# Low score product of a two-part attention kernel: full-height zero-padded matmuls replaced by half-height row tiles of TensorE

## Chip, cores, metric

The kernel runs on one core of one Trainium2 chip. The metric is the device time of one execution in microseconds; the runs before the change gave a median of 685.42 us (three runs, 685.2 to 685.59). The profile is one further execution, taken by the hardware profiler.

## What is computed

One layer of a streaming encoder: layer norm with a modulation, one input projection, two attention branches of 8 heads each, a gate, one output projection, a residual and a second layer norm. Sequence length and width are 1024, the head dimension 64, the query block 128, all in float32. Cut to the two branches around the change (`ke` is the number of keys that query block `i` sees):

```python
for i in range(8):
    qs, ke = i * 128, (i + 1) * 128
    # stick-breaking branch
    z = einsum('bhqd,bhkd->bhqk', q[:, :, qs:ke], k[:, :, :ke]) * 64 ** -0.5
    log_keep = where(strict, log_sigmoid(-z), 0)
    later = cumsum(log_keep, reverse=True) - log_keep
    w = where(strict, exp(log_sigmoid(z) + later), 0);  out = w @ v
    # forgetting branch
    s = einsum(...) * 64 ** -0.5 + (f_q[:, None] - f_k[None, :])
    out = softmax(where(causal, s, -inf)) @ v
```

## The kernel before

**Two-part numbers.** Most matmuls here take their operands in a rounded float32 type (`fp32r`). To keep the accuracy, the kernel splits each operand in a rounded high part and the rest, the low part, and adds up products of the parts: high times high, low times high, high times low.

**Pairs and units.** The 16 heads are treated as 8 pairs `p` of two heads `h`; pairs 0 to 3 are the stick-breaking heads, 4 to 7 the forgetting ones. A *unit* is `(p, h, i)`: one head and one block of 128 queries, with `ke = 128 * (i + 1)` keys, 128 units in all. Half of them (`i` of 0 to 3) have at most 512 keys, half have 640, 768, 896 or 1024.

**Where q and k stand.** For each head, `qst[p][h]` and `kst[p][h]` are tiles of 128 partitions by 1024 columns. `evac_q` (L265) puts the high part of q on the partition half of its own head, `r`, and the low part on the other half, `o`. `evac_k` (L274) puts the high part of k on half `r`, copies it by a DMA to half `o`, and writes the low part to `klo[p]`, one tile for both heads, each on its own half and at its own key columns (L284). One product of 128 rows, `qst` by `kst`, then gives high q by high k plus low q by high k at once (L459).

**The low product before.** What is left is high q by low k. `klo[p]` holds both heads, one on each half, so the stationary operand is a padded tile: `qz[h][b]` (two buffers per head) is cleared at the start (L104), and `att_query` (L428) copies the high q of the unit, 64 partitions by 128 columns, to the half of its head (L433, on ScalarE, 128 times). The other half stays zero, and a 128-row product (L460) with `klo[p]` gives the head's share alone.

**How a unit goes.** `att_scores` (L447) writes the scores of a unit to `S`, a PSUM tile of two banks of 512 columns, of which there is one. Up to 512 keys take one bank. More keys are cut into two equal halves, one per bank: width 320, 384, 448 or 512 each, in the order high, low, high, low. Then ScalarE takes the sigmoids `kp` and `be` from S (L481, L483; pairs 0 to 3), or VectorE takes the masked sum and maximum (L467; pairs 4 to 7). VectorE scans `kp` (L488), or ScalarE takes the exponential (L472); POOL multiplies (L494, L475). Two units later, PE transposes the weights in blocks of 128 (L511), ScalarE and VectorE split them in two parts (L513, L514), and PE multiplies them by v (L528).

**What sets the order.** On PE the order is the written one: after each unit's scores come projection matmuls of later pairs as fillers (L296 to L298, L354 to L356; a table `FILL` says how many steps per pair), transposes and products with v. Near the end the fillers are the output projection (L913 to L915). On SP the order is written by hand for the start. On ScalarE, VectorE and POOL a scheduler of the framework sets it from its own model of time. In pair 4 and later, the forget gates' row sums are transposed once by a matmul that uses 64 columns of the array (L411, tile `frow`).

Of the kernel before, what the change touches and what calls it, by code (L numbers as in the profile page):

```python
# [8 lines left out]
F32 = mybir.dt.float32  # L9
F32R = mybir.dt.float32r  # L10
AF = mybir.ActivationFunctionType
ALU = mybir.AluOpType

P = 128
# [4 lines left out]
HD = 64  # L19
# [8 lines left out]
def tile_hybrid_layer(  # L28
# [17 lines left out]
    nc = tc.nc  # L46
# [9 lines left out]
    def att_tile(name, dt=F32):  # L56
        return big("att", 6, name, dt)
# [13 lines left out]
    def s_tile(name):  # L71
        return ps.tile([P, 2, 512], F32, tag="S", bufs=1, name=name)
# [10 lines left out]
    def after(*instructions):  # L83
        stack = ExitStack()
        for i in instructions:
            stack.enter_context(tc.issue_after(i.ins))
        return stack
# [11 lines left out]
    nc.gpsimd.memset(half.bitcast(F32), 0.5)  # L99

    qz = [[cp.tile([P, P], F32R, tag=f"qz{h}{b}", name=f"qz{h}{b}") for b in range(2)] for h in range(2)]
    for h in range(2):
        for t in qz[h]:
            nc.gpsimd.memset(t.bitcast(F32), 0.0)  # L104
    gate = cp.tile([P, D], F32, tag="gate", name="gate")
    mhalf = cp.tile([P, 1], F32, tag="mhalf", name="mhalf")
    nc.gpsimd.memset(mhalf, -0.5)
# [73 lines left out]
    for kt in range(NB):  # L181
        nc.tensor.matmul(sc_all[:, kt // 4, kt % 4 * P:][:, :P], sc[:, kt:kt + 1].to_broadcast([P, P]), ident,
                         start=True, stop=True)
# [90 lines left out]
    def evac_k(p, ch, acc, kst, klo, heads):  # L274
        s = slice(ch * 512, ch * 512 + 512)
        for h in heads:
            r = slice(h * HD, h * HD + HD)
            o = slice((1 - h) * HD, (1 - h) * HD + HD)
            first = nc.scalar.copy(kst[h][r, s], acc[r, :])
            if ch == 1 and p in (2, 4, 6):  # L280
                key_casts[:] = [first]
            kf = kst[h].bitcast(F32)
            nc.sync.dma_start(kf[o, s], kf[r, s])
            last = nc.vector.tensor_tensor(klo[r, s], acc[r, :], kf[r, s], op=ALU.subtract)  # L284
        return first, last

    def evac_g(p, ch, acc, sg):
# [12 lines left out]
    qst, kst, klo, sgt, vt = {}, {}, {}, {}, {}  # L300
# [12 lines left out]
    def evac_m(p, m, ch, acc, heads=(0, 1)):  # L313
        if m == 0:
            evac_q(p, ch, acc, qst[p], heads)
        elif m == 1:
            return evac_k(p, ch, acc, kst[p], klo[p], heads)
        else:
            evac_g(p, ch, acc, sgt[p])
# [108 lines left out]
    def att_query(u):  # L428
        p, h, i = u
        zq[u] = z = qz[h][turn[h] % 2]  # L430
        turn[h] += 1
        r = slice(h * HD, h * HD + HD)
        nc.scalar.copy(z[r, :], qst[p][h].bitcast(F32)[r, i * P:i * P + P])  # L433

    masks, scaled, lows = [], [], []

    def att_causal(u):
        p, h, i = u
        if p >= 4:
            if not masks:  # L440
                masks.append(pv_tile("causal_ps", 1)[:, :P])
                nc.vector.tensor_copy(masks[0], causal)
            f = fb[2 * (p - 4) + h]
            dg = slice(i * P, i * P + P)
            nc.vector.tensor_tensor(f[:, dg], f[:, dg], masks[0], op=ALU.add)

    def att_scores(u, following):  # L447
        p, h, i = u
        z = zq.pop(u)
        ke = (i + 1) * P  # L450
        ns = 1 if ke <= 512 else 2
        w = ke // ns
        qs = slice(i * P, i * P + P)
        if p >= 4:
            f = fb[2 * (p - 4) + h]
        S = s_tile(f"S_{p}_{h}_{i}")
        for s in range(ns):
            ks = slice(s * w, s * w + w)
            nc.tensor.matmul(S[:, s, :w], qst[p][h][:, qs], kst[p][h][:, ks], start=True, stop=False)  # L459
            nc.tensor.matmul(S[:, s, :w], z, klo[p][:, ks], start=False, stop=True)  # L460
        v3 = lambda a: a[:, :ke].rearrange("p (a b) -> p a b", a=ns)
        if p >= 4:
            a = att_tile(f"a_{p}_{h}_{i}")
            nm = sb.tile([P, 1], F32, tag="nm", bufs=4, name=f"nm_{p}_{h}_{i}")
            l = sb.tile([P, 1], F32, tag="l", bufs=4, name=f"l_{p}_{h}_{i}")
            with after(*lows):
                nc.vector.tensor_tensor_reduce(out=v3(a), in0=S[:, :ns, :w], in1=v3(f),  # L467
                                               op0=ALU.add, op1=ALU.min, scale=-1.0, scalar=BIG,
                                               accum_out=nm)
            if following:  # L470
                att_causal(following)
            nc.scalar.activation(a[:, :ke], a[:, :ke], AF.Exp, scale=-1.0, bias=nm, accum_out=l)  # L472
            nc.vector.reciprocal(l, l)  # L473
            scaled[:] = [*scaled[-3:],
                         nc.gpsimd.tensor_scalar(a[:, :ke], a[:, :ke], l, 1.0, op0=ALU.mult, op1=ALU.mult)]  # L475
            st_w[u] = a
        else:
            kp = att_tile(f"kp_{p}_{h}_{i}")
            be = att_tile(f"be_{p}_{h}_{i}")
            with after(*key_casts):  # L480
                nc.scalar.activation(v3(kp), S[:, :ns, :w], AF.Sigmoid, scale=-1.0)  # L481
            key_casts.clear()
            last_act = nc.scalar.activation(v3(be), S[:, :ns, :w], AF.Sigmoid)  # L483


            lo = max(ke - 512, 0)
            rv = kp[:, lo:ke][:, ::-1]
            last_dve = nc.vector.tensor_tensor_scan(rv, rv, floor[:, :ke - lo], initial=0.0,  # L488
                                                    op0=ALU.mult, op1=ALU.max)
            if lo:  # L490
                rv = kp[:, :lo][:, ::-1]
                last_dve = nc.vector.tensor_tensor_scan(rv, rv, floor[:, P:P + 1].to_broadcast([P, lo]),  # L492
                                                        initial=kp[:, lo:lo + 1], op0=ALU.mult, op1=ALU.max)
            nc.gpsimd.tensor_tensor(be[:, :ke - 1], be[:, :ke - 1], kp[:, 1:ke], op=ALU.mult)  # L494
            nc.gpsimd.memset(be[:, ke - 1:ke], 0.0)
            st_w[u] = be
            return last_act, last_dve
# [182 lines left out]
    for kb in range(NB):  # L680
        last = kb == NB - 1
# [17 lines left out]
        else:  # L699
            parts = range(2 if kb + 2 < NB else 0)  # L700
# [110 lines left out]
    for kb in range(NB):  # L811
# [9 lines left out]
        if kb < len(evacs):  # L821
            n, h = evacs[kb]
# [6 lines left out]
    last = nc.vector.tensor_copy(held[:, 512:], acc1[1])  # L829
# [230 lines left out]
    def scores_turn(k):  # L1060
        if k < len(units):
            if k == 16 * 4 - 1:
                load_fb(0)
                load_fb(1)
            if k == 0:
                att_query(units[0])
            issued = att_scores(units[k], units[k + 1] if k + 1 < len(units) else None)
            if k == 16 * 4 - 1:
                att_causal(units[k + 1])
            if k in HELD:  # L1070
                m, h = HELD[k]
                with after(*issued):
                    evac_m(0, m, 1, held[:, m * 512:(m + 1) * 512], (h,))
            with after(*(issued or ())):
                while summed:
                    att_sum(*summed.pop(0))
            if k + 1 < len(units):
                att_query(units[k + 1])
            p, h, i = units[k]
            if 4 <= p < NPAIR - 1 and i == 0:  # L1080
                load_fb(2 * (p - 4) + h + 2)
# [83 lines left out]
```

## Time and profile before

| what | value |
|---|---|
| median of 3 runs | 685.42 us (685.2 to 685.59) |
| the profiled execution's own time | 685.27 us |
| its span, first to last instruction | 683.2 us |
| mean granted TensorE clock | 0.998 |
| instructions | 11185 |
| matmuls and weight loads | 3713 each |
| HBM | 60.34 MB read, 16.29 MB written |

PE is the row of matmuls, PEld that of the loads of stationary operands, which run beside PE. DVE is VectorE, ACT ScalarE, POOL GpSimd. In a timeline row stand start and length in us, engine, line, operation, the tile written and the tiles read, then `rows*columns` of the array and the moving operand, whose second number is the width. Matmuls are pipelined: the next one can start before the record of the last one ends. The chain that ended last follows the work back from the last instruction, at each step to what released it.

### The profile page before, as it was taken

How to read it: one execution, taken by the hardware profiler on the slowest of the kernel's cores; microseconds unless marked ns; L12 is line 12 of the kernel's file. 1: busy time of each engine (PE TensorE's matmuls, PEld its weight loads, DVE VectorE, ACT ScalarE, POOL GpSimd, SP SyncE). 2: the span in 40 equal slices, each digit the busy share in tenths (PEclk: the TensorE clock that was granted, in tenths of full speed). 3: DMA queues.
4: the chain of work that ended last, by engine and by line, in shares of the span. 5: the costliest groups of instructions: out<-in, count | busy, mean ns of one | idle time of the engine just before them, and what ended most of it. 6: DMA issues, size and time to landing. Idle time of an engine off the chain costs nothing.

```text
span 683.2 us, 11185 instructions
## 1 busy us (share of the span) xinstructions
PE 670.8 (98%) x3713; PEld 571.9 (84%) x3713; DVE 485.1 (71%) x996; ACT 379.1 (55%) x857; POOL 404.6 (59%) x529
## 2 busy tenths in 40 slices
PE   8999999999999999999999999999999999999995
PEld 4788898888998888889988888889988888888885
DVE  6697779878666777786776675766676777875645
ACT  5567377756567666575665565655565666521000
POOL 5560179756357656566378878777785365655411
PEclk9999999999999999999999999999999999999999
DMA  9973422112102121122123455254352297143301
GB/s 330 410 274 141 140 74 79 29 39 59 32 15 65 45 64 42 40 54 55 49 92 129 166 161 169 79 173 147 117 163 73 61 356 300 59 178 104 119 32 61
DMA packets 45272, 81.54 MB, mean 119 GB/s; under 512 B 5216, under 2 KB 19360, under 8 KB 44960
## 3 DMA queue, kind: packets, MB, share of 16 engines
q1 hardware_dynamic: 43632, 76.54, 34.3%
q10 hardware_dynamic: 1584, 4.31, 1.9%
q8 instruction: 29, 0.48, 0.3%
q14 instruction: 27, 0.22, 0.1%
HBM read 60.34 MB, written 16.29 MB: 112 GB/s over the span
## 4 chain that ended last, share of the span: by engine, by line
PE 91%; DVE 2%; POOL 2%; ACT 2%; issue 1%; DMA 1%; SPq 0%; DVEq 0%; POOLq 0%; ACTq 0%
PE m L296 10%; PE m L298 10%; PE m L297 9%; PE pv L528 9%; PE T L511 9%; PE S L459 5%; PE S L460 5%; PE o L915 4%; PE o L913 4%; PE o L914 4%; PE v L356 4%; PE v L354 4%; PE v L355 4%; PE st_q L620 1%; PE st_late L620 1%
## 5 line engine op out<-in xcount | busy, mean ns | idle before, releaser
L514 DVE TENSOR_TENSOR pt<-T,pt 128x512 fp32r<-128x512 f32 (+2 forms) x192 | 102.8, 552 | 31.6 <-ACT pt L513 30.0
L296 PE MATMUL m<-uh,whi 128*128 128x512 f32 x304 | 122.8, 404 | 0.0
L513 ACT CAST pt<-T 128x512 fp32r<-128x512 f32 (+2 forms) x192 | 88.7, 478 | 58.9 <-PE T L511 54.9
L298 PE MATMUL m<-uh,wlo 128*128 128x512 f32 x304 | 119.7, 394 | 0.0
L297 PE MATMUL m<-ul,whi 128*128 128x512 f32 x304 | 119.6, 393 | 0.0
L494 POOL TENSOR_TENSOR be<-be,kp 128x127 f32<-128x127 f32 (+3 forms) x64 | 78.4, 1226 | 37.0 <-DVE kp L492 23.9
L488 DVE TENSOR_TENSOR_SCAN kp<-kp,floor 128x512 f32<-128x512 f32 (+2 forms) x64 | 65.0, 1015 | 26.3 <-ACT kp L481 25.1
L528 PE MATMUL pv<-pt,v 128*128 128x512 f32 x320 | 82.8, 389 | 0.0
L459 PE MATMUL S<-k,q 128*128 128x512 f32 (+5 forms) x192 | 69.4, 363 | 0.3 <-DVE nm L467 0.2
L475 POOL TENSOR_SCALAR a<-a,l 128x1024 f32<-128x1024 f32 (+3 forms) x64 | 48.1, 752 | 36.4 <-DVE l L473 26.8
L298 PEld LDWEIGHTS m<-uh,wlo 128*128 128x128 f32 x304 | 57.1, 188 | 13.7
L296 PEld LDWEIGHTS m<-uh,whi 128*128 128x128 f32 x304 | 57.1, 188 | 10.2
L460 PE MATMUL S<-kl,qz 128*128 128x512 f32 (+5 forms) x192 | 65.3, 341 | 0.0
L297 PEld LDWEIGHTS m<-ul,whi 128*128 128x128 f32 x304 | 57.2, 188 | 9.4
L472 ACT ACTIVATE a<-a,nm 128x1024 f32<-128x1024 f32 (+3 forms) x64 | 49.8, 778 | 26.7 <-DVE nm L467 26.1
L528 PEld LDWEIGHTS pv<-pt,v 128*128 128x128 f32 x320 | 55.5, 189 | 9.0
L544 POOL TENSOR_TENSOR ty<-ty,sg 64x256 f32<-64x256 f32 x64 | 47.0, 734 | 23.3 <-DVE ty L543 10.0
L467 DVE CUSTOM_DVE_ANT_0 a<-S,fb 128x1024 f32<-128x1024 f32 (+3 forms) x64 | 48.2, 753 | 16.2 <-PE S L460 12.0
L433 ACT CAST qz<-q 64x128 fp32r<-64x128 f32 x128 | 37.3, 296 | 34.1 <-PE S L460 32.8
L356 PE MATMUL v<-wlo_v,uh 128*128 128x256 f32 (+1 forms) x192 | 54.4, 283 | 0.8 <-POOL wlo_v L127 0.8
L354 PE MATMUL v<-whi_v,uh 128*128 128x256 f32 (+1 forms) x192 | 54.7, 285 | 0.0
L355 PE MATMUL v<-whi_v,ul 128*128 128x256 f32 (+1 forms) x192 | 54.1, 282 | 0.0
(290 smaller groups left out, 1609.8 us busy)
## 6 DMA issues: line engine op xcount, KB each, us to landing
raw<-in_w_qkg_dram SPq DMA_DIRECT2D x38, 256.0 KB, 2.7
wss<-in_w_ss_dram SPq DMA_DIRECT2D x12, 512.0 KB, 8.5
x<-in_x_dram SPq DMA_DIRECT2D x8, 512.0 KB, 7.3
k<-k SPq DMA_DIRECT2D x32, 128.0 KB, 2.3
wg<-in_w_gate_dram SPq DMA_DIRECT2D x8, 512.0 KB, 5.0
raw_o<-in_w_out_dram SPq DMA_DIRECT2D x16, 256.0 KB, 3.0
fb<-f_dr ACTq DMA_DIRECT2D x8, 512.0 KB, 4.3
wo_dr<-whi_o SPq DMA_DIRECT2D x16, 256.0 KB, 2.2
```

Of the source, the lines that this page charges most:

```text
L296: nc.tensor.matmul(acc, hi[:, c], u_hi[kt][:, s], start=(kt == 0), stop=False)
L297: nc.tensor.matmul(acc, hi[:, c], u_lo[kt][:, s], start=False, stop=False)
L298: nc.tensor.matmul(acc, lo[:, c], u_hi[kt][:, s], start=False, stop=(kt == NB - 1))
L354: nc.tensor.matmul(acc[:, :n], u_hi[kt][:, ts_], hi[:, s], start=(kt == 0), stop=False)
L355: nc.tensor.matmul(acc[:, :n], u_lo[kt][:, ts_], hi[:, s], start=False, stop=False)
L356: nc.tensor.matmul(acc[:, :n], u_hi[kt][:, ts_], lo[:, s], start=False, stop=(kt == NB - 1))
L459: nc.tensor.matmul(S[:, s, :w], qst[p][h][:, qs], kst[p][h][:, ks], start=True, stop=False)
L460: nc.tensor.matmul(S[:, s, :w], z, klo[p][:, ks], start=False, stop=True)
L494: nc.gpsimd.tensor_tensor(be[:, :ke - 1], be[:, :ke - 1], kp[:, 1:ke], op=ALU.mult)
L513: nc.scalar.copy(hi[:, :n, qo:qo + P], t3)
L514: lows[:] = [nc.vector.tensor_tensor(lo[:, :n, qo:qo + P], t3, hi.bitcast(F32)[:, :n, qo:qo + P], op=ALU.subtract)]
L528: nc.tensor.matmul(acc2[:, :, q0:], vt[p][:, kb, h * P:(h + 1) * P], pt[:, :, q0:], start=(kb == 0), stop=(kb == last))
```

## The change

1. `klo[p]` is laid out by key half: head `h` takes columns `512 h` to `512 h + 511`, with its first 512 keys on partitions 0 to 63 and the other 512 on partitions 64 to 127.
2. More than 512 keys are cut into 512 and the rest (128, 256, 384 or 512), no longer into equal halves; the columns of S are now contiguous.
3. All high products of a unit come first, then the low ones. A low product has 64 rows: for key part `s` those of partition half `s`. On the head's own half (`s == h`) the stationary operand is `qst` itself; on the other it is a copy of the high q, moved to that half.
4. `att_query` makes that copy only where it is needed: not for head 0 with `i` below 4, whose keys all lie in part 0. So 96 of the 128 copies stay. The padding is gone, and with it the four memsets.

```diff
-    for h in range(2):
-        for t in qz[h]:
-            nc.gpsimd.memset(t.bitcast(F32), 0.0)
...
-            last = nc.vector.tensor_tensor(klo[r, s], acc[r, :], kf[r, s], op=ALU.subtract)
+            last = nc.vector.tensor_tensor(klo[ch * HD:ch * HD + HD, h * 512:h * 512 + 512], acc[r, :], kf[r, s],
+                                           op=ALU.subtract)
...
+        if h == 0 and i < 4:
+            return
         r = slice(h * HD, h * HD + HD)
-        nc.scalar.copy(z[r, :], qst[p][h].bitcast(F32)[r, i * P:i * P + P])
+        o = slice((1 - h) * HD, (1 - h) * HD + HD)
+        nc.scalar.copy(z[o, :], qst[p][h].bitcast(F32)[r, i * P:i * P + P])
...
-        for s in range(ns):
-            ks = slice(s * w, s * w + w)
-            nc.tensor.matmul(S[:, s, :w], qst[p][h][:, qs], kst[p][h][:, ks], start=True, stop=False)
-            nc.tensor.matmul(S[:, s, :w], z, klo[p][:, ks], start=False, stop=True)
-        v3 = lambda a: a[:, :ke].rearrange("p (a b) -> p a b", a=ns)
+        parts = [(s, min(512, ke - s * 512)) for s in range(2 if ke > 512 else 1)]
+        for s, n in parts:
+            nc.tensor.matmul(S[:, s, :n], qst[p][h][:, qs], kst[p][h][:, s * 512:s * 512 + n], start=True, stop=False)
+        for s, n in parts:
+            r = slice(s * HD, s * HD + HD)
+            nc.tensor.matmul(S[:, s, :n], (qst[p][h][:, qs] if s == h else z)[r], klo[p][r, h * 512:h * 512 + n],
+                             start=False, stop=True)
+        S = S.rearrange("p a b -> p (a b)")[:, :ke]
...
-                nc.scalar.activation(v3(kp), S[:, :ns, :w], AF.Sigmoid, scale=-1.0)
+                nc.scalar.activation(kp[:, :ke], S, AF.Sigmoid, scale=-1.0)
```

**The order on PE.** Here stand the rows of pair 0, head 0, from the last product with v to the next filler, before the change, for the unit of 640 keys. A name ends in its head, its block and a buffer number. `S_0_4_1208` is the score tile of head 0, block 4; `k`, `q`, `kl` and `qz` are `kst`, `qst`, `klo` and the padded tile; the last entry is the moving operand's size by rows that reach the output.

```order
L528 MATMUL pv_1_0_1205<-pt_1_0_0_1115,v_519 128x2x128
L459 MATMUL S_0_4_1208<-k_0_254,q_0_252 128x320
L460 MATMUL S_0_4_1208<-kl_256,qz_80 128x320
L459 MATMUL S_0_4_1208<-k_0_254,q_0_252 128x320
L460 MATMUL S_0_4_1208<-kl_256,qz_80 128x320
L354 MATMUL v_7_1181<-whi_v_2b,uh_128 128x256
```

The same place after the change (line numbers and buffer numbers are those of the changed kernel):

```order
L530 MATMUL pv_1_0_1197<-pt_1_0_0_1107,v_515 128x2x128
L458 MATMUL S_0_4_1200<-k_0_250,q_0_248 128x512
L458 MATMUL S_0_4_1200<-k_0_250,q_0_248 128x128
L461 MATMUL S_0_4_1200<-kl_252,q_0_248 128x512
L461 MATMUL S_0_4_1200<-kl_252,qz_80 128x128
L352 MATMUL v_7_1173<-whi_v_2b,uh_124 128x256
```

Only the four score products moved and changed their widths; what stands ahead of them and behind them is the same, here and in every other unit. The two `kl` rows are those of 64 rows each.

**The order on ScalarE.** Pair 0, head 1, block 4 before the change: `pt` is the split of transposed weights, `kp` and `be` the sigmoids of S, `ty` a step of the output sum, `qz` the copy of q into the buffer that the low product of this unit reads last; it is for the unit two blocks on.

```order
L513 CAST pt_0_3_1_1386<-T_0_6_1_1387 128x3x128
L481 ACTIVATE kp_1_4_1398<-S_1_4_1393 128x640
L483 ACTIVATE be_1_4_1399<-S_1_4_1393 128x640
L541 COPY ty_0_2_1406<-pv_0_2_1379 64x256
L433 CAST qz_82<-q_1_253 64x128
L513 CAST pt_0_3_0_1371<-T_0_7_0_1426 128x4x128
```

And after it:

```order
L515 CAST pt_0_3_1_1378<-T_0_6_1_1379 128x3x128
L434 CAST qz_82<-q_1_249 64x128
L483 ACTIVATE kp_1_4_1390<-S_1_4_1385 128x640
L485 ACTIVATE be_1_4_1391<-S_1_4_1385 128x640
L543 COPY ty_0_2_1398<-pv_0_2_1371 64x256
L515 CAST pt_0_3_0_1363<-T_0_7_0_1418 128x4x128
```

The copy of q moved from behind the sigmoids of this unit to ahead of them; it does so in nearly all long units of pairs 0 to 3. 32 copies are gone. The orders on SP, VectorE and POOL stay as they were, but for the memsets and three swaps of neighbours.

More of the change, by code (lines that the diff above doesn't have):

```diff
@@ L450, in att_scores @@
         ke = (i + 1) * P
-        ns = 1 if ke <= 512 else 2
-        w = ke // ns
         qs = slice(i * P, i * P + P)
@@ L466, in att_scores @@
             with after(*lows):
-                nc.vector.tensor_tensor_reduce(out=v3(a), in0=S[:, :ns, :w], in1=v3(f),
+                nc.vector.tensor_tensor_reduce(out=a[:, :ke], in0=S, in1=f[:, :ke],
                                                op0=ALU.add, op1=ALU.min, scale=-1.0, scalar=BIG,
@@ L480, in att_scores @@
             with after(*key_casts):
-                nc.scalar.activation(v3(kp), S[:, :ns, :w], AF.Sigmoid, scale=-1.0)
+                nc.scalar.activation(kp[:, :ke], S, AF.Sigmoid, scale=-1.0)
             key_casts.clear()
-            last_act = nc.scalar.activation(v3(be), S[:, :ns, :w], AF.Sigmoid)
+            last_act = nc.scalar.activation(be[:, :ke], S, AF.Sigmoid)
             lo = max(ke - 512, 0)
```

## The prediction

> **What bounds the kernel now.** I read the page first: busy time by engine, then the chain that ended last.
>
> ```profile
> PE 670.8 (98%) x3713; PEld 571.9 (84%) x3713; DVE 485.1 (71%) x996; ACT 379.1 (55%) x857; POOL 404.6 (59%) x529
> PE 91%; DVE 2%; POOL 2%; ACT 2%; issue 1%; DMA 1%; SPq 0%; DVEq 0%; POOLq 0%; ACTq 0%
> ```
>
> TensorE is busy 98% of the span and holds 91% of the chain. Busy time alone could hide gaps, because a matmul's record is longer than the time it blocks the next one. So I read the waits of PE, and the busy time of every engine in the attention stretch.
>
> ```profile
> PE sc_all L176 <- POOL ident masks.py:199: 1.5, 1, 1.5
> PE v L356 <- POOL wlo_v L127: 0.8, 1, 0.8
> PE S L459 <- DVE nm L467: 0.2, 1, 0.2
> 81.00:575.00 494.00, 492.23 (x2835) 427.63 (x2834) 356.12 (x745) 310.42 (x724) 326.23 (x408) 1.00 0.33 100
> ```
>
> In the 494 us from 81 to 575 PE is busy 492.23, DVE 356.12 (72%), ACT 310.42 (63%), POOL 326.23 (66%), at a granted clock of 1.00. The longest wait of PE there is 0.8 us, once, on a weight split on POOL. So what shortens PE's own stream there should shorten the run almost one for one, and what lengthens it is paid in full.
>
> The price of a matmul is therefore the distance between two starts. Here is one score unit of 1024 keys, then the ends of one of 896 keys and one of 768, then one of 640. Columns: start in us, length in us, engine, line.
>
> ```profile
> 345.17 0.39 PE L459 MATMUL S<-k,q 128*128 128x512 f32 x1
> 345.40 0.40 PE L460 MATMUL S<-kl,qz 128*128 128x512 f32 x1
> 345.63 0.39 PE L459 MATMUL S<-k,q 128*128 128x512 f32 x1
> 345.86 0.39 PE L460 MATMUL S<-kl,qz 128*128 128x512 f32 x1
> 346.09 0.39 PE L296 MATMUL m<-uh,whi 128*128 128x512 f32 x1
> ...
> 350.93 0.36 PE L459 MATMUL S<-k,q 128*128 128x448 f32 x1
> ...
> 351.74 0.39 PE L296 MATMUL m<-uh,whi 128*128 128x512 f32 x1
> ...
> 355.39 0.34 PE L459 MATMUL S<-k,q 128*128 128x384 f32 x1
> ...
> 356.09 0.39 PE L296 MATMUL m<-uh,whi 128*128 128x512 f32 x1
> ...
> 362.90 0.31 PE L459 MATMUL S<-k,q 128*128 128x320 f32 x1
> ...
> 363.48 0.39 PE L296 MATMUL m<-uh,whi 128*128 128x512 f32 x1
> ```
>
> A 512-wide matmul lasts 0.39 us, but the next one starts after 0.23. The four products of a unit block PE for 0.92 us at 1024 keys, 0.81 at 896, 0.70 at 768 and 0.58 at 640: together 3.01 us per head. Each is four times the price of its width (0.230, 0.2025, 0.175, 0.145), with nothing lost between the products.
>
> Narrow ones need two more rows: a 256-wide product with its successor, and eight 128-wide transposes on the chain.
>
> ```profile
> 374.98 0.28 PE L459 MATMUL S<-k,q 128*128 128x256 f32 x1
> 375.10 0.28 PE L460 MATMUL S<-kl,qz 128*128 128x256 f32 x1
> 375.21 0.39 PE L296 MATMUL m<-uh,whi 128*128 128x512 f32 x1
> 125.45 0.87 PE T L511 x8
> ```
>
> 256 columns cost 0.115 us. Transposes of 128 columns follow each other every 0.87/8 = 0.11, hardly less than 256, so I take 0.11 as the least distance between two matmuls with different weights.
>
> **The main term: units of more than 512 keys** (4 per head, 64 in all). The four products are cut anew, into 512 and the rest n = 128, 256, 384, 512, and put in the order high, high, low, low. The two high products cost 0.23 and 0.11, 0.115, 0.175 or 0.23. The two low ones now use 64 rows each, on different halves of the array, and write different banks of S. If they run side by side, the pair costs as much as its longer member, 0.23. New cost: 0.57 + 0.575 + 0.635 + 0.69 = 2.47 us per head, against 3.01: 0.54 less, and over 16 heads **8.6 us less**.
>
> No matmul of this trace uses part of the rows, so side by side isn't shown here, and this cost has two ends. At the other end the pair runs one after the other: 0.68 + 0.69 + 0.81 + 0.92 = 3.10 per head, 0.09 more than now (a 128-wide product is paid as 0.11), which is 1.4 us more. Between them, the second low product's weights might load only once the first has started; then the pair takes 0.23, 0.23, 0.285 or 0.34, which gives back 0.165 per head, 2.6 us in all. I take the full overlap: the pair has disjoint rows and banks, and weight loads overlap running matmuls throughout (row below). The Trainium skill (TensorE: Matmul & The Clock Gate, Part 3) says that matmuls in distinct row groups run concurrently with starts about 4 ns apart; no row here can show it.
>
> **The switch of array shape.** All 128 units now have a 128-row product, then one or two of 64 rows, then 128-row work again: 128 times in and out. The nearest row is one transposition of the forget gates that uses 64 of the columns. It stands between a 512-wide product and 128-wide transposes. PE first, then its weight loads.
>
> ```profile
> 229.61 0.40 PE L298 MATMUL m<-uh,wlo 128*128 128x512 f32 x1
> 229.84 0.28 PE L411 MATMUL frow<-ident,fc 128*64 128x128 f32 x1
> 229.96 0.60 PE L511 MATMUL T<-ident,be 128*128 128x128 f32 x4
> ```
> ```profile
> 229.61 0.11 PEld L411 LDWEIGHTS frow<-ident,fc 128*64 128x64 f32 x1
> 229.84 0.47 PEld L511 LDWEIGHTS T<-ident,be 128*128 128x128 f32 x4
> ```
>
> In and out take 0.35 us, where 0.23 + 0.11 = 0.34 would be paid without a switch. The load for the narrow tile ran while the wide matmul was in flight. So 0.01 us per unit is my value: 128 x 0.01 = **1.3 us more**. Lower end: 0. Upper end: PE empties at each switch, so that a 512-wide matmul blocks its whole recorded 0.39 and not 0.23, 0.16 more, twice per unit: 128 x 0.32 = 41 us. I take the low value because this row is the only change of shape in the trace. It changes columns, not rows, which is why the upper end stays a rival. The Trainium skill (TensorEngine Tiling (Array Packing), Key Properties) states that changing the tiling mode, not just the tile, drains TensorE. This row doesn't agree; by that rule the sum would be the upper end's.
>
> **What is absorbed.** PE's 0.8 us wait at 457 hangs on POOL and a weight DMA. What PE gains just before it, one 1024-key unit at 452.6, becomes a longer wait: 0.23 us lost.
>
> **Edits that cost nothing on the path.** 32 copies of q into a padded tile go (head 0, the four short units, 8 pairs); the other 96 stay and change only the half they write.
>
> ```profile
> L433 ACT CAST qz<-q x128: 281/296/305, 45.1 to 592.4; 64x128 fp32r<-64x128 f32 x128
> ACT qz L433 <- PE S L460: 32.8, 36, 2.0
> ACT kp L481 <- PE S L460: 19.1, 22, 2.1
> PE T L511 <- POOL be L494: 0.4, 1, 0.4
> L284 DVE TENSOR_TENSOR kl<-m,k x24: 656/689/696, 159.5 to 548.5; 64x512 fp32r<-64x512 f32 x24
> L271 DVE SCALAR_TENSOR_TENSOR q<-m,q x24: 683/688/694, 143.1 to 528.6; 64x512 fp32r<-64x512 f32 x24
> 1.73 0.64 POOL L104 MEMSET qz<- 128x128 f32 x4
> 4.67 0.20 POOL L169 TENSOR_TENSOR sc<-cm,c_sb 128x8 f32<-128x8 f32 x1 [2.14 <-ACT cm L168]
> ```
>
> That frees 32 x 296 ns = 9.5 us of ACT, which mostly waited for S around these copies (32.8 and 19.1 us). ACT has 2% of the chain, and 9.5 is 2.5% of its 379 busy us, so at most 0.3 us of the span; I count 0 and keep 0.3 for the range. In the first four pairs the long units' copy now stands ahead of the sigmoids on S and waits for the low product that frees its buffer. Behind it on ACT the two sigmoids are queued, up to 0.3 us later, and for them wait DVE's scan and POOL's product, which PE transposes two units later. PE waited for that product 0.4 us in all, so the slack of two units hides it; without that cover 32 long units would lose 32 x 0.3 = 9.6 us, which 688.5 still holds. The low part of k goes to the other partition half in half of its 32 writes: L271 crosses halves already and takes 688 ns where L284 takes 689, so nothing. The four memsets (0.64 us) lie before a POOL wait of 2.14 for ACT. The consumers of S read as many elements as before and still wait for the last low product.
>
> **Sum** against the profiled execution's own 685.27 us (span 683.2 and 2.07 around it): 685.27 - 8.6 + 1.3 + 0.2 = **678.2 us**. The median of the runs, 685.42, is 0.15 above it, within their spread of 0.4, so I leave it there. About 0.2%, 1.4 us, is what a measurement can tell from no change.
>
> **Rivals.** *No overlap* (chance 0.15). The low pair runs one after the other: 685.27 + 1.4 + 1.3 = 688.0. Against it: loads run beside matmuls. For it: no row shows two matmuls streaming at once.
>
> *The switch drains the array* (0.20, on the slower side). The place is the first 64-row product after a 128-row one, and the first 128-row matmul after it. The mechanism: results of a 64-row tile might leave the array earlier than those of 128 rows still in flight to the same bank, so the array must empty first; the column switch above wouldn't show that. It decides from (8.6 - 0.2)/128 = 0.066 us per unit. One full drain per unit, 0.16, gives 685.27 - 8.4 + 20.5 = 697.4; two give 718. A partial drain of 0.03 to 0.10 gives 681 to 690, both signs. Of the 0.20, 0.04 falls on faster, 0.03 on same, 0.13 on slower. Its chance is no larger because the one switch in the trace costs 0.01. It is what the Trainium skill's rule above (TensorEngine Tiling (Array Packing), Key Properties) would do here.
>
> *The second load waits* (0.10): 678.2 + 2.6 = 680.8, still faster.
>
> *Hidden anyway* (0.05): DVE at 72% or POOL at 66% takes over, and the run stays near 685. Against it: PE hardly waits for either.
>
> **Chances.** Forecast 0.50, rivals 0.15, 0.20, 0.10, 0.05. Faster: 0.50 + 0.10 + 0.04 = 0.64; same: 0.05 + 0.03 = 0.08; slower: 0.15 + 0.13 = 0.28. The forecast's own range is 676.0 to 680.8: no switch cost at all, the 0.3 of ACT and the runs' spread below, the late load above. The full range reaches to no overlap, 688.0, and 0.5 of spread: 676.0 to 688.5; left out are mainly the drains above 0.09 per unit.
>
> **What the profile after would show.** Right: in a 1024-key unit the two low products start within 0.02 us of each other, and the next matmul comes 0.69 us after the unit's first, not 0.92; after a short unit the next comes no later than before. No overlap: low starts 0.23 apart. Late load: 0.11 apart. Drain: the first low product starts over 0.3 us after a 512-wide high one, or the one behind the pair is late, in short units as well. Hidden: unit times as forecast, but longer waits of PE for DVE or POOL. The forecast fails above all if the row switch costs more than 0.066 us per unit.

## The result, and the profile after

The changed kernel took 719.40 us against 685.31 before: a ratio of 1.0498 (95% interval 1.0478 to 1.0519), **34 us slower**. The forecast was 678.2, in a range of 676.0 to 688.5. The execution that was profiled first took 2350.69 us, so the profile shown is of a second measurement of the same kernel (719.42 us, span 717.7).

The page of the changed kernel, busy time by engine and the chain by engine, and then all its waits of PE.

```profile
PE 708.0 (99%) x3713; PEld 561.4 (78%) x3713; DVE 487.1 (68%) x996; ACT 371.8 (52%) x825; POOL 404.3 (56%) x525
PE 97%; ACT 1%; DVE 1%; issue 0%; POOL 0%; DVEq 0%; POOLq 0%
```
```profile
PE sc_all L173 <- POOL ident masks.py:199: 1.5, 1, 1.5
PE st_q L622 <- ACT hw L608: 0.4, 1, 0.4
PE st_q L622 <- ACT uh L252: 0.3, 1, 0.3
PE st_q L622 <- POOL hw L609: 0.2, 1, 0.2
```

PE is still the bound, more than before: 97% of the chain where it had 91%, and the waits that are left belong to the start of the program; those in the attention stretch are gone. It executes as many matmuls as before and, past the start, waits for nobody, yet needs 34 us more. So the loss lies between the starts of its own matmuls.

PE's timeline in the changed kernel, a unit of 1024 keys and the two matmuls behind it, then the loads of its low pair. (`x2` merges the two high products; lengths are in the second column.)

```profile
549.65 0.62 PE L458 MATMUL S<-k,q 128*128 128x512 f32 x2
550.20 0.49 PE L461 MATMUL S<-kl,qz 64*128 64x512 f32 x1
550.20 0.50 PE L461 MATMUL S<-kl,q 64*128 64x512 f32 x1
550.63 0.50 PE L294 MATMUL m<-uh,whi 128*128 128x512 f32 x1
550.97 0.39 PE L295 MATMUL m<-ul,whi 128*128 128x512 f32 x1
```
```profile
550.20 0.18 PEld L461 LDWEIGHTS S<-kl,qz 64*128 64x128 f32 x1 [0.36 <-issue]
550.20 0.18 PEld L461 LDWEIGHTS S<-kl,q 64*128 64x128 f32 x1
```

The pair overlaps: both low products start in the same hundredth of a microsecond, and so do their loads. But the two high ones take 0.55 and not 0.46, the pair 0.43 and not 0.23, and the first matmul behind it 0.34 and not 0.23. From 549.65 to 550.97 are 1.32 us. Five starts of the kernel before would be 5 x 0.23 = 1.15, and the forecast was 0.69 + 0.23 = 0.92: 0.40 too little.

The same in a short unit of 512 keys, where nothing overlaps; PE first, then its weight loads.

```profile
565.14 0.39 PE L296 MATMUL m<-uh,wlo 128*128 128x512 f32 x1
565.37 0.40 PE L458 MATMUL S<-k,q 128*128 128x512 f32 x1
565.70 0.49 PE L461 MATMUL S<-kl,qz 64*128 64x512 f32 x1
566.12 0.50 PE L294 MATMUL m<-uh,whi 128*128 128x512 f32 x1
566.46 0.40 PE L295 MATMUL m<-ul,whi 128*128 128x512 f32 x1
```
```profile
565.14 0.19 PEld L458 LDWEIGHTS S<-k,q 128*128 128x128 f32 x1
565.70 0.18 PEld L461 LDWEIGHTS S<-kl,qz 64*128 64x128 f32 x1 [0.36 <-issue]
566.12 0.19 PEld L294 LDWEIGHTS m<-uh,whi 128*128 128x128 f32 x1 [0.24 <-issue]
566.23 0.19 PEld L295 LDWEIGHTS m<-ul,whi 128*128 128x128 f32 x1
```

The loads tell how. Those of the high product (L458) start at 565.14, with the matmul ahead of it, and are hidden. Those of the 64-row product start only at 565.70, 0.33 after the start of the high product, and the record of the product itself grows from 0.39 to 0.49. On the way back the same: the loads of L294 start at 566.12, 0.42 after the low product's start, and those of the next one 0.11 later. From 565.37 to 566.46 are 1.09 us, where three starts cost 0.69: 0.40 lost to one change in and one out. By these starts each change costs about 0.09 until the loads begin and about 0.10 in which a load runs and nothing covers it.

### The profile page after: what moved, and what is told of

The parts are those of the page before. It is cut to its first block, busy times and chain, and to the rows that moved or that the text cites. A ratio compares the mean times of both kernels' runs of the same rounds, so it can differ in the third digit from the quotient of the medians.

```text
span 2349.0 us, 11168 instructions
## 1 busy us (share of the span) xinstructions
PE 2340.3 (100%) x3713; PEld 1370.4 (58%) x3713; DVE 499.1 (21%) x996; ACT 380.9 (16%) x825; POOL 403.4 (17%) x525
## 4 chain that ended last, share of the span: by engine, by line
PE 99%; issue 1%; DVE 0%; POOL 0%; DVEq 0%; POOLq 0%
PE m L294 11%; PE m L295 11%; PE m L296 11%; PE T L513 10%; PE pv L530 10%; PE S L458 5%; PE o L917 5%; PE o L915 5%; PE o L916 4%; PE v L352 4%; PE v L354 4%; PE v L353 4%; PE S L461 3%; PE st_late L622 1%; PE st_k L622 1%; PE st_q L622 1%
## 5 line engine op out<-in xcount | busy, mean ns | idle before, releaser
L294 PE MATMUL m<-uh,whi 128*128 128x512 f32 x304 | 330.9, 1088 | 0.0
L295 PE MATMUL m<-ul,whi 128*128 128x512 f32 x304 | 329.1, 1082 | 0.0
L296 PE MATMUL m<-uh,wlo 128*128 128x512 f32 x304 | 328.9, 1082 | 0.0
L530 PE MATMUL pv<-pt,v 128*128 128x512 f32 x320 | 270.2, 1060 | 0.0
L294 PEld LDWEIGHTS m<-uh,whi 128*128 128x128 f32 x304 | 107.2, 353 | 134.0 <-issue 129.8
L458 PE MATMUL S<-k,q 128*128 128x512 f32 (+2 forms) x192 | 168.1, 967 | 0.0
L513 PE MATMUL T<-ident,be 128*128 128x128 f32 x288 | 142.4, 710 | 0.0
L513 PE MATMUL T<-ident,a 128*128 128x128 f32 x288 | 137.1, 679 | 0.0
L915 PE MATMUL o<-woh,whi_y 128*128 128x512 f32 (+2 forms) x119 | 128.2, 1077 | 0.0
L917 PE MATMUL o<-wol,whi_y 128*128 128x512 f32 (+2 forms) x119 | 125.6, 1055 | 0.0
L916 PE MATMUL o<-woh,wlo_y 128*128 128x512 f32 (+2 forms) x119 | 125.6, 1055 | 0.0
```

Source lines behind the costliest of these rows:

```text
L294: nc.tensor.matmul(acc, hi[:, c], u_hi[kt][:, s], start=(kt == 0), stop=False)
L295: nc.tensor.matmul(acc, hi[:, c], u_lo[kt][:, s], start=False, stop=False)
L296: nc.tensor.matmul(acc, lo[:, c], u_hi[kt][:, s], start=False, stop=(kt == NB - 1))
L458: nc.tensor.matmul(S[:, s, :n], qst[p][h][:, qs], kst[p][h][:, s * 512:s * 512 + n], start=True, stop=False)
L513: nc.tensor.transpose(tp[:, b * P:(b + 1) * P], a[:, kb * P:(kb + 1) * P], ident)
L530: nc.tensor.matmul(acc2[:, :, q0:], vt[p][:, kb, h * P:(h + 1) * P], pt[:, :, q0:], start=(kb == 0), stop=(kb == last))
```

## The experiments

Theory A: a change between 128-row and 64-row products costs 0.3 to 0.4 us in and out, while the pair does overlap. Rivals: 64-row products are themselves slow (B), or nothing overlaps (C), or the new cut or order brings the loss. The times stand against runs of the kernel before from the same chip: 685.23 us for experiments 1 to 4, 685.47 us for 5 to 8.

**1. The changed kernel again** (no edit).

> The changed kernel once more, for a profile at its usual time. All theories: 719.4 us. Theory A (TensorE empties at each change between 128-row and 64-row products, and the two low products of a long unit still overlap): (719.4 - 685.3 + 8.4) / 128 = 0.33 us per unit; in the trace the first low product starts about 0.39 us after a 512-wide high one and not 0.23, the two low ones within 0.02 us, and the next full-height matmul about 0.39 us after the low ones. Theory B (64-row products run at half rate, one after the other, and switching is free): the low products of a 1024-key unit start 0.46 us apart, and the first of them 0.23 us after the last high one. Theory C (switching costs, and the pair does not overlap): (34.1 - 1.4) / 128 = 0.255 us per unit, low products 0.23 us or more apart.

Measured: 719.43 us against 685.23, ratio 1.0497 (1.048 to 1.0515). The trace above decides: the first low product comes 0.33 after a 512-wide high one, the pair starts together, and the next full-height matmul comes 0.43 after it. B and C fail on the common start of the pair. A had the sizes partly wrong: 0.39 was expected on each side of the pair, and a third delay, on the matmul behind the next one, wasn't foreseen.

**2. Only the low products cut to 64 rows, high, high, low, low.**

```diff
...
-        nc.scalar.copy(z[r, :], qst[p][h].bitcast(F32)[r, i * P:i * P + P])
...
+        own = slice(h * HD, h * HD + HD)
...
-            nc.tensor.matmul(S[:, s, :w], z, klo[p][:, ks], start=False, stop=True)
+        for s in range(ns):
+            ks = slice(s * w, s * w + w)
+            nc.tensor.matmul(S[:, s, :w], qst[p][h][own, qs], klo[p][own, ks], start=False, stop=True)
```

> The kernel before, with the low product cut to the 64 rows that are not zero: both low products of a long unit stand on the same partition half, behind the two high ones; equal halves and the layout of k's low part as before, no padded tiles and copies. No overlap is possible, and TensorE changes shape 128 times in and out, as in the changed kernel. Theory A: 685.3 + 128 x 0.33 = 727.8 us. Theory B: every low product twice as long: 685.3 + 34 = 719.4 us. Theory C: 685.3 + 128 x 0.255 = 718 us.

Measured: 729.28 us, ratio 1.0641 (1.0625 to 1.0657). 44.05 us for 128 changes in and out, 0.344 us each. This is close to A's 727.8 and clear of B's 719.4 and C's 718. It is 9.85 us above the changed kernel, which has as many changes but overlaps its pairs. The copies of q are gone altogether here and k's low part stands as before, so neither can be the cause.

**3. The same, high, low, high, low.**

```diff
...
+        own = slice(h * HD, h * HD + HD)
...
-            nc.tensor.matmul(S[:, s, :w], z, klo[p][:, ks], start=False, stop=True)
+            nc.tensor.matmul(S[:, s, :w], qst[p][h][own, qs], klo[p][own, ks], start=False, stop=True)
```

> As row64_hhll, but in the order high, low, high, low, so that the 64 long units change shape twice: 192 times in and out. Theory A: 685.3 + 192 x 0.33 = 749 us, 21 us more than row64_hhll. Theory B: no difference from row64_hhll, 719.4 us. Theory C: 685.3 + 192 x 0.255 = 734 us.

Measured: 753.69 us, ratio 1.0996 (1.098 to 1.1013). Against experiment 2 nothing but the order differs, and 64 more changes in and out cost 24.41 us: 0.381 each, where A had 0.33 and so 749 us. PE's timeline of this kernel in a 1024-key unit:

```profile
375.83 0.48 PE L456 MATMUL S<-k,q 128*128 128x512 f32 x1
376.24 0.50 PE L457 MATMUL S<-kl,q 64*128 64x512 f32 x1
376.67 0.50 PE L456 MATMUL S<-k,q 128*128 128x512 f32 x1
377.10 0.49 PE L457 MATMUL S<-kl,q 64*128 64x512 f32 x1
377.52 0.38 PE L351 MATMUL v<-whi_v,uh 128*128 128x256 f32 x1
```

The last three products, the full-height one too, have another shape ahead of them and block PE for 0.42 to 0.43 us instead of 0.23. The first stands behind transposes of its own shape; its 0.41 holds the way in of the second. B, by which this run equals experiment 2, is out.

**4. Only the new cut and order**, low products with 128 rows and padding.

```diff
...
+        for s, n in parts:
+            nc.tensor.matmul(S[:, s, :n], z, klo[p][:, s * 512:s * 512 + n], start=False, stop=True)
```

> The kernel before with only the new cut (512 and the rest) and the new order (high, high, low, low); the low products keep 128 rows and the zero padding. All theories: the 640-key units pay a 128-wide product as 0.11 instead of 0.06, about 0.09 us per head, 685.3 + 1.4 = 686.7 us. If the cut or the order itself had brought the loss, it would show here as 719 us.

Measured: 686.87 us, ratio 1.0023 (1.0014 to 1.0033). 1.6 us, as all theories had it: the cut and the order carry next to nothing of the loss.

**5. Changes in columns instead of rows**: in the kernel before, a 64-column transposition of the identity ahead of each group of transposes, overwritten by them.

```diff
             tp = t_tile(f"T_{p}_{h}_{i}_{g}")
+            nc.tensor.transpose(tp[:HD, :P], ident[:, :HD], ident)
```

> The kernel before with one more matmul ahead of each group of weight transposes: a transposition of 64 columns of the identity into the group's own PSUM tile, which the real transposes then overwrite. It uses 64 columns and all 128 rows of the array, 192 times. Theory A (a change in the number of rows of the tile costs about 0.09 us for the array to run empty and about 0.105 us for a weight load that is no longer hidden, twice per unit; a change in columns costs nothing, as the one row of the profile before showed): 192 x 0.11 = 21 us for the work itself, 706 us. Rival (every change of shape costs 0.38 us in and out, and the single row of before misled): 192 x 0.38 = 73 us on top, 779 us.

Measured: 701.95 us against 685.47, ratio 1.0235 (1.022 to 1.0251). 16.5 us for 192 added matmuls, 0.086 each, less than the 0.11 set for their work (706 us were expected) and far from the rival's 779 us. PE's timeline of this kernel around one of them, then its loads:

```profile
303.25 0.39 PE L298 MATMUL m<-uh,wlo 128*128 128x512 f32 x1
303.48 0.27 PE L509 MATMUL T<-ident 128*64 128x128 f32 x1
303.59 0.60 PE L512 MATMUL T<-ident,be 128*128 128x128 f32 x4
```
```profile
303.25 0.11 PEld L509 LDWEIGHTS T<-ident 128*64 128x64 f32 x1
303.48 0.47 PEld L512 LDWEIGHTS T<-ident,be 128*128 128x128 f32 x4
```

The loads of the narrow tile start with the wide matmul ahead of it, and those of the wide one with the narrow one. So a change in columns costs nothing that can be seen. The row on which the prediction leaned was right for what it showed, and did not show what was asked.

**6. Fewer rows in use, in the same tile**: the low products of head 0 with 96 rows, which the program still places in a tile of 128.

```diff
-            nc.tensor.matmul(S[:, s, :w], z, klo[p][:, ks], start=False, stop=True)
+            r = slice(0, P - 32) if h == 0 else slice(0, P)
+            nc.tensor.matmul(S[:, s, :w], z[r], klo[p][r, ks], start=False, stop=True)
```

> The kernel before, where the low products of head 0 use 96 of the 128 rows (its own 64 and 32 of the zero padding), in the order high, low, high, low; the program still gives them a tile of 128 rows. Theory A (it is the tile's shape that costs, not the number of rows in use): 685.3 us, no change. Rival (each change in the number of rows in use costs): 32 short units once and 32 long units twice, 96 times 0.38 us, 722 us.

Measured: 685.72 us against 685.47, ratio 1.0001 (0.9992 to 1.001). 96 changes in the number of rows in use cost nothing. In a unit of 1024 keys the load of a 96-row product starts with the 128-row product ahead of it:

```profile
306.85 0.39 PE L459 MATMUL S<-k,q 128*128 128x512 f32 x1
306.85 0.19 PEld L461 LDWEIGHTS S<-kl,qz 96*128 96x128 f32 x1
```

The trace lists these products by their 96 rows; that their tile has 128 is taken from the program, and no view shows it. If so, it is the height of the tile that counts, and not the rows in use.

**7. The pair twice**, so that the long units add their low part twice.

```diff
+        times = len(parts)
+        for d in range(times):
+            for s, n in parts:
...
-                             start=False, stop=True)
+                                 start=False, stop=(d == times - 1))
```

> The changed kernel with the pair of low products of each long unit issued twice in a row, so that the low part is added twice there; nothing else differs. Theory A (inside one shape a pair costs its longer member, 0.23 us, with loads hidden): 64 x 0.23 = 14.8 us more than the changed kernel, 734 us. Rival 1 (the weight load of the second pair is not hidden either): 64 x 0.33 = 21 us more, 741 us. Rival 2 (the pair starts together but streams one after the other): 16 x 1.56 = 25 us more, 744 us.

Measured: 734.83 us, ratio 1.0714 (1.0696 to 1.0732). That is 49.36 us over its own reference, where the changed kernel is 34.20 over its own: 15.2 us for 64 more pairs, 0.237 each. Inside one shape a pair costs its longer member. In this kernel's timeline, a unit of 768 keys (`x2` merges the two 256-wide ones):

```profile
356.90 0.49 PE L463 MATMUL S<-kl,qz 64*128 64x512 f32 x1
356.90 0.50 PE L463 MATMUL S<-kl,q 64*128 64x256 f32 x2
357.23 0.39 PE L463 MATMUL S<-kl,qz 64*128 64x512 f32 x1
357.56 0.38 PE L352 MATMUL v<-whi_v,uh 128*128 128x256 f32 x1
```

The first 512-wide product blocks 0.33 (0.23 plus an uncovered load), the second 0.33 (0.23 plus the way out): together 0.66, where one pair alone takes 0.43 (the 1024-key unit above).

**8. Row tiles in the long units alone**, padded 128-row products in the short ones.

```diff
...
+        if i < 4:
+            zq[u] = z = qpad[turn[2] % 2]
+            turn[2] += 1
+            nc.scalar.copy(z[:HD, :], qst[p][h].bitcast(F32)[r, i * P:i * P + P])
+            return
...
+            if ke <= 512:
+                nc.tensor.matmul(S[:, s, :n], z, klo[p][:, h * 512:h * 512 + n], start=False, stop=True)
+                continue
...
```

The left-out lines clear the padded tiles `qpad` and the other half of the first `klo`, and let both heads share two buffers for the moved copies.

> The changed kernel with row tiles in the long units alone; the low product of the short units is one of 128 rows again, with a padded copy of q over the new layout of k's low part. 64 changes of shape in and out instead of 128, and only where a pair hides something. Theory A: the short units cost 0.33 (128 keys) to 0.39 us each by the starts in the trace, about 0.36 with those before transposes: 719.4 - 64 x 0.36 = 696.4 us, still slower than before, since what a pair hides (at most 0.23) is less than 0.39. Rival (the loss is made by the pairs in the long units): it stays above 710 us.

Measured: 698.90 us, ratio 1.0187 (1.0168 to 1.0205). Of the 34.2 us, 20.8 go with the 64 short units, 0.325 each (0.36 was expected, and 696.4 us). The loss is no matter of the pairs: without the change of shape in half of the units it falls by more than half. The rest, 13.4 us, is 64 changes less what the pairs hide (64 x 0.344 - 8.6 = 13.4).

## Why the prediction was wrong

**What bounds the kernel: right.** PE alone; the 34 us show up in its own starts, and no other engine took over or was exposed. *Hidden anyway* is out.

**The main term, 8.6 us less: right.** The pair starts together, and a pair costs its longer member (0.237 us per added one in experiment 7, against 0.23). Experiments 1 and 2, with and without overlap, differ by 9.85 us. *No overlap* is out. So is *the second load waits*: the two loads of a pair start together as well.

**The switch of array shape, 1.3 us more: this is the step that failed.** "0.01 us per unit is my value" was taken from one change in columns. With the main term at its 8.6, the switch measures (34.2 + 8.6) / 128 = 0.334 us per unit, 43 us in place of 1.3. Experiment 2 gives 0.344 without any overlap, experiment 3 0.381 for 64 more. The shown units lose 0.40. The mean is lower for two reasons, which a comparison of all matmul starts in the traces of before and of experiment 2 shows. Units of 128 keys lose 0.29 us, those of 256 keys 0.36, longer ones 0.37 to 0.39, about 47 us in all; and about 3 us come back outside the units, 0.95 of it at the one wait of 0.8 us that PE had on a weight split. Experiment 5 shows that the column row was sound, and that it doesn't carry over to rows.

The rival *the switch drains the array* was the right one. Its upper end, two full drains of 0.16 at 718 us, lies 1.4 us from the result, but that closeness is partly luck. The rows show a wait of about 0.09 before the loads begin and 0.10 of loads that nothing covers, at each change, not 0.16 of pipeline. Its mechanism, results in flight to the same bank, isn't what the runs show either. In the short unit the low product follows a high one into the same bank, 0.33 behind it (565.70 - 565.37); in the long unit the first low product follows one into the other bank, and the delay is the same (0.55 - 0.23 = 0.32). On the way back the late matmul writes another tile, `m`. The chance of 0.20 was too low: the prediction itself noted that columns aren't rows, and then weighed the row as if they were. The Trainium skill (TensorEngine Tiling (Array Packing), Key Properties) states that changing the tiling mode drains TensorE. The 64-row products agree, with 0.34 to 0.38 us in and out; the 64-column ones, at 0.086 us each with their work, do not. That TensorE is quite empty in between isn't shown: the load at 565.70 starts before the record of the product ahead ends at 565.77, an end that is modelled. Why the loads wait stays open.

**The edits costed at nothing: right as far as they were tried.** The cut cost 1.6 us (1.4 forecast, in the serial case). The copy of q ahead of the sigmoids, the new layout of the low part and the memsets weren't tried alone, but PE waits for nothing behind them, and experiment 2 loses as much per change without the copies and with the old layout.

No version with row tiles beats the kernel before. A pair hides at most 0.23 us, a change in and out costs 0.34 to 0.38. Two pairs of 512 in one shape would, by these prices, hide 0.46; that needs four banks for scores, and wasn't tried.

## What to carry to other kernels

Before cutting a matmul into row tiles, count how often TensorE must change between tile heights, and price each change in and out, which cost about 0.35 us here: what the overlap hides per visit has to exceed that, by estimate some 770 columns (0.344 us at 0.23 us per 512). Stay in the shape for several pairs, or leave the zeros in: here a padded product that streams in step with its neighbours was cheaper than a smaller one that breaks their step. When the trace of before has only a near relative of the new operation, and the two ends of its price differ by the whole gain, the ends belong in the chances as well.

## What the runs showed of the hardware

- Two products of 64 rows on different halves of the array, into different PSUM banks, start in the same hundredth of a microsecond and cost as much as the longer one (0.237 us for 512 columns).
- In these traces weight loads run under the matmul ahead when both have the same tile height: 128 rows behind 128 (load and matmul ahead both at 565.14), 64 behind 64 (experiment 7: the second pair's loads start at 357.00, the first pair at 356.90). Behind a change of height the first load starts 0.33 us after a 512-wide matmul or 0.42 us after a 64-row one, and runs uncovered, in both directions; full-height matmuls too are paid as 0.43 instead of 0.23 us.
- A change from 128 to 64 columns and back costs nothing that can be seen (0.086 us per added matmul, its work included), and neither do products of 96 rows among those of 128 (685.72 against 685.47 us).
